# A scan's hand-written stage order: new letters, output finishes that run across stages, output transposes in the state's PSUM banks

## The chip, the cores and the metric

The kernel runs on one core of a Trainium2 chip. The metric is device microseconds of one execution. TensorE (PE) does the matrix products, VectorE (DVE) and ScalarE (ACT) read their results out of PSUM, GpSimd (POOL) works in SBUF alone, and SyncE (SP) issues nearly all DMAs. Each engine works its own instructions off in order and waits on semaphores for the others.

## The reference

One layer of a bidirectional mixer: 128 context tokens and 2048 latent tokens of width 1024. A norm and one input projection feed two head groups. Group B is a short gated convolution. Group A has 8 heads of 64 channels and runs a delta-rule state update once forward and once backward; the two results are added, normalised per head, gated, concatenated with group B and sent through one output projection.

```python
def step(S, inp):
    r_t, w_t, k_t, v_t, kk_t, a_t = inp
    s_kk = jnp.einsum('bdhij,bdhj->bdhi', S, kk_t)
    S = (S * w_t[..., None, :] - s_kk[..., :, None] * (kk_t * a_t)[..., None, :]
         + v_t[..., :, None] * k_t[..., None, :])
    return S, jnp.einsum('bdhij,bdhj->bdhi', S, r_t)
...
y = ys[:, 0] + jnp.flip(ys[:, 1], axis=1)
```

## The kernel before

`phase1` computes the projections and spills the operands of the scan to device memory, `phase2` is the scan, `phase3` the output projection. The change is in `phase2`.

The scan works on chunks of 64 tokens. A stage takes one pair of heads `p` and eight chunks per direction: group 0 is forward, group 1 backward. There are 17 stages: for each of four head pairs the four blocks b = 0 to 3 (the forward group takes block b, the backward group block 3 - b), and the context as stage 15. So stages 0 to 3 are b = 0 to 3 of the first head pair, 4 to 7 of the second, 8 to 11 of the third. Inside a stage `partS` makes eight steps. Step i multiplies the state with the chunk's matrix (psS, L1002), for group 0 and then group 1, and VectorE scales the new state into `sv` (L1015). This chain is serial: psS of the next step needs `sv` of this one.

Everything else in a stage is preparation for later stages or the end of earlier ones. It is cut into parts, which are generators or functions:

- `partL` loads the operands `rr` of a stage (1 MB per group, two buffers in all) four stages ahead.
- `partM`, three stages ahead, makes six pieces in the order of `MORD`: per group G with D (product psG, two masked copies to GA by VectorE, then `dg`), Q (transposes psQ, two ScalarE copies) and F (product psF, two ScalarE copies and two VectorE masks). All of them use a PSUM pool of two banks, and a piece takes both.
- `partI` transposes `dg` on VectorE (L852) and lets GpSimd solve the small triangular systems (L857 to L871).
- `partZ`, two stages ahead, transposes the solution on VectorE (L917, L920) and copies it into `zb` with four ScalarE copies. `partU`, one stage ahead, makes psU and psW with the ScalarE copies `bu` and the negated `zb`.
- `partW` and `partw`, one stage ahead, stack operands by eight ScalarE copies and load the rest. `partB` makes psX (eight ScalarE copies into `fs`) and then the chunk matrices psE with VectorE's masks into `E` (L965). `partm` takes the mean out of a new head pair's start state.
- `outputs` reads the upper half of a psS bank, after steps 3 and 7: a ScalarE copy (L719) at the first visit to `y`, which is in b = 0 and 1, a VectorE addition (L1032) at the second, in b = 2 and 3. Two output blocks are complete at the end of each b = 2 and b = 3.
- `finish` ends a completed block in pieces, one for each `f`: fetch `sg` and Square (ScalarE, L1063); the sum (VectorE, L1066); the root (ScalarE, L1068); reciprocal, multiply and the fetch of `q` (VectorE, L1070 and L1071); the transposes psT (TensorE, L1083) and their scaling (L1086); the addition (L1088) and the store to `mixT`.

What is written between the steps is set by strings: the eight strings of `ORDER`, one for each step, list the parts in the order in which they are issued after the step's own psS and `sv`. `b` is the rest of this stage's `partB`, `B` the start of the next one's; `M`, `W`, `U`, `I`, `Z`, `l`, `r`, `w`, `m`, `f` are the parts above. For stages 0 to 13 the instructions of TensorE, VectorE and ScalarE stand in exactly this order (`manual_schedule`). GpSimd's and SyncE's are placed by the planner, as are all of the last three stages, whose strings are in `LAST` and into which the output projection is woven.

PSUM has eight banks: two for `partM` and half of psX (`O.pm`), two for psU, psW, psX, psE and psT (`O.p2`), four for psS (`O.pS`), where two are taken at step 0 and two at step 4, each until `outputs` has read it.

Of the kernel before, what the change touches and what calls it, by code (L numbers as in the profile page):

```python
# [6 lines left out]
F32 = mybir.dt.float32  # L7
# [610 lines left out]


NST = 17  # L620
MORD = (("GD", 0), ("Q", 0), ("GD", 1), ("F", 0), ("Q", 1), ("F", 1))
ON_DVE = ""
LA = 3


ORDER = ("WbMUf", "WbMbMf", "fMUIlwf", "MfMr", "Bff", "Bfm", "ffZf", "Bf")
LAST = ("bUf", "bbWwf", "fWUf", "f", "Bff", "Bfm", "ffZf", "Bf")


def phase2(K):  # L630
    nc, tc, A, S = K.nc, K.tc, K.A, K.S
# [3 lines left out]
    B = Ctx()  # L635
    O = Ctx()
# [275 lines left out]
    def partZ(s, st):  # L912

        zr = st.zr = tl([128, 16, 32], "zr", 1, O.l1)
        zd = st.zd = tl([128, 16, 32], "zd", 1, O.l1)
        zb = B.zb
        r = V.transpose(zr[:].rearrange("p u (q h) -> p q h u", h=2), st.zt[:].rearrange("p q i -> p (q i)"))  # L917
        if O.scaled is not None:
            tc.add_manual_dep(r.ins, O.scaled.name, mybir.DependencyInfo(mybir.DependencyClass.NoSync, mybir.DependencyReason.DATA), reason="order")
        V.transpose(zd[:], zr[:])  # L920
        for r0, r1 in rows:
            copy("z", zb[r0, :, 0:32], zd[r0])
            copy("z", zb[r1, :, 32:64], zd[r1])
# [46 lines left out]
    sts = {}  # L970
    held = {}
    pend = []

    def partS(s, st, nxt):

        sp = {}
        for i in range(8):
            for gi, g in enumerate(st.g):
# [4 lines left out]
                p, c = g.units[u]  # L983
# [9 lines left out]
                m, q = (u % 2, u // 2) if ctx else (u // 4, u % 4)  # L993
# [23 lines left out]
                    if ctx and lastc:  # L1017
                        D(S["nst"][:, d, 2 * p:2 * p + 2, :], so[:])
                if i % 4 == 3:
                    outputs(g.units[0][0], g.blk, m, sp[gi])  # L1020
            yield

    def outputs(p, blk, m, ps):
# [16 lines left out]
    def finish(p, blk, y):  # L1040
# [31 lines left out]
        q = tl([128, 512], "w", 1)  # L1072
        fetch("q", q)
        yield
        pt = O.p2.tile([128, 512], F32, tag="s", name=f"psT{K.u()}")
        idm = B.idt[:]
        for i in range(4):
            if blk is None:
# [12 lines left out]
        else:  # L1091
            D(S["mixT"][p * 128:(p + 1) * 128, t0:t0 + 512], o[:])
        K.mixed[blk] = K.mixed.get(blk, 0) + 1
        yield

    K.mixed = {}

# [10 lines left out]
    def main():  # L1108
        setup_rest()
        run = lambda gen: [None for _ in gen]  # L1110
        partZ(0, sts[0])
        run(partW(0, sts[0]))
        partw(0, sts[0])
        partm(0, sts[0])
        run(first(2))
        partL(LA)
        run(partU(0, sts[0]))
        bb = partB(0, sts[0])
        for _ in range(3):
            next(bb)  # L1120
        partZ(1, sts[1])
        tail = iter(())
        order = tc.manual_schedule(engines={mybir.EngineType.PE, mybir.EngineType.DVE, mybir.EngineType.Activation})
        for s in range(NST):
            if s == 0:
                order.__enter__()
            if s == NST - 3:
                order.__exit__(None, None, None)
            st = sts.pop(s)
            nxt = sts.get(s + 1)  # L1130
            todo = [pend.pop(0) for _ in range(len(pend))]
            if s == NST - 3:
                O.pm.close()
                O.r2.close()
                O.r1.close()
                K.weights()
# [12 lines left out]
            for i, _ in enumerate(partS(s, st, nxt)):  # L1149
                next(tail, None)  # L1150
                for c in (ORDER if s < NST - 3 else LAST)[i]:
                    if c in gens:
                        next(gens[c], None)
                    elif c in "lr" and s + LA + 1 < NST:
                        partL(s + LA + 1, ("lr".index(c),))
                    elif c == "I" and s + LA < NST:
                        partI(s + LA, sts[s + LA])
                    elif c == "w" and nxt:
                        partw(s + 1, nxt)
                    elif c == "m" and nxt:  # L1160
                        partm(s + 1, nxt)
                    elif c == "Z" and s + 2 < NST:
                        partZ(s + 2, sts[s + 2])
                    elif c == "f":
                        while todo and next(todo[0], 1):
                            todo.pop(0)
            for f in todo:
                run(f)
        for f in pend:
            for _ in f:  # L1170
                pass
        for p in (O.pS, O.p2):
            p.close()
        K.rest(tail)
        for p in (O.l0, O.rI, O.r0):
            p.close()
# [190 lines left out]
```

## Time and profile before

| | us |
|---|---|
| median of 3 runs | 1763.87 (1762.28 to 1771.26) |
| profiled execution, its own time | 1767.54 |
| its span, first to last instruction | 1765.6 |
| up to the first psS of stage 0 | 1047.15 |
| stages 0 to 13 | 443.87 |
| stages 14 to 16 | 120.08 |
| from the last psS to the end | 154.50 |

The page of the profile names each group of instructions by line, engine, operation and the tiles it writes and reads. In the rows of a window view, each engine's busy time is followed by its number of instructions in brackets. In a row of the waits stand who waited, for whom, the time in total, how often and the longest. In a row of the timeline stand start, duration, engine, line and, in brackets, how long the engine was idle before and what ended it. A wait for several semaphores is put down to the one that came last.

### The profile page before, as it was taken

The page shows a single profiled execution, that of the slowest core. Times are in us where ns is not written, and L with a number is a line of the kernel's source. Part 1 is how long each engine was busy: PE and PEld are TensorE (multiplying, and loading weights), DVE is VectorE, ACT ScalarE, POOL GpSimd, SP SyncE. Part 2 cuts the span into 40 slices and gives each one's busy share as a digit, 9 for nine tenths or more (in the row PEclk, how much of TensorE's full clock was granted, in tenths as well). Part 3 has the DMA queues.
Part 4 walks back from the last instruction along what each step waited for, and adds up shares of the span by engine and source line. Part 5 has one row for each costly group of instructions (what it writes and reads, how often), then busy time and mean ns, then how long its engine had stood idle before and what let it go on. Part 6 is the DMA issues. An engine that isn't in the chain of part 4 may idle for free.

```text
span 1765.6 us, 42096 instructions
## 1 busy us (share of the span) xinstructions
PE 1588.2 (90%) x17364; PEld 1447.4 (82%) x17364; DVE 1126.3 (64%) x2099; ACT 776.9 (44%) x1539; POOL 586.4 (33%) x1053
## 2 busy tenths in 40 slices
PE   5998999999899999999999988978878878889998
PEld 2998899899888899989899977767767767677886
DVE  5998887545787626378854255776766766466433
ACT  4565644224444303255511155756556556442222
POOL 0122210001122100012208157876876776212221
PEclk8999999999899999999999968988989988989999
DMA  9788787565787744477785345455554654345442
GB/s 364 218 244 233 233 255 250 200 239 133 160 194 176 191 166 143 152 178 196 212 287 199 118 117 155 121 165 140 141 158 115 154 150 116 110 137 193 153 143 90
DMA packets 204271, 313.43 MB, mean 178 GB/s; under 512 B 58024, under 2 KB 147496, under 8 KB 190000
## 3 DMA queue, kind: packets, MB, share of 16 engines
q1 hardware_dynamic: 168496, 310.61, 58.5%
q10 hardware_dynamic: 35584, 0.14, 1.3%
q8 instruction: 136, 2.23, 0.5%
q14 instruction: 55, 0.45, 0.1%
HBM read 207.79 MB, written 102.91 MB: 176 GB/s over the span
## 4 chain that ended last, share of the span: by engine, by line
PE 44%; DVE 9%; ACT 6%; DMA 5%; issue 2%; POOL 0%; SPq 0%; DVEq 0%; ACTq 0%
PE psE L964 6%; PE psu L1240 3%; PE psu L1242 3%; DMA scr_ops<-sp 3%; PE psu L1241 3%; PE psS L1002 3%; PE psF L817 2%; ACT stf L717 2%; PE psX L950 2%; PE psG L817 2%; DVE ab L852 1%; PE psT L1083 1%; PE mmb L159 1%; PE mmb L160 1%; PE mmb L158 1%
## 5 line engine op out<-in xcount | busy, mean ns | idle before, releaser
L871 POOL TENSOR_TENSOR zt<-zt,ztmp 128x30 f32<-128x30 f32 (+7 forms) x510 | 202.3, 397 | 38.7
L868 POOL TENSOR_TENSOR ztmp<-ab,zt 128x60 f32<-128x60 f32 (+7 forms) x255 | 134.5, 527 | 19.2
L965 DVE TENSOR_TENSOR E<-psE,msk 128x512 f32<-128x512 f32 x136 | 93.0, 689 | 54.7 <-PE psE L964 54.3
L1002 PE MATMUL psS<-sv,E 128*64 128x64 f32 x2176 | 107.9, 242 | 18.7 <-DVE E L965 12.0
L1002 PEld LDWEIGHTS psS<-sv,E 128*64 128x64 f32 x2176 | 87.7, 150 | 41.5 <-DVE E L965 16.1
L314 POOL TENSOR_TENSOR shk<-rawl 128x384 f32<-128x384 f32 (+1 forms) x24 | 20.0, 833 | 279.8 <-ACT rawl L310 269.4
L717 ACT ACTIVATE stf<-psX 64x512 f32<-64x512 f32 x136 | 80.3, 590 | 35.5 <-PE psX L950 32.6
L1015 DVE TENSOR_TENSOR sv<-psS,pc 64x128 f32<-64x128 f32 x254 | 63.5, 274 | 45.5 <-PE psS L1002 44.8
L1303 POOL TENSOR_TENSOR z<-z,x 128x512 f32<-128x512 f32 x32 | 41.5, 1297 | 137.7 <-DVE z L1299 111.3
L158 PE MATMUL mmv<-h,w 128*128 128x384 f32 (+1 forms) x192 | 69.4, 361 | 18.9 <-ACT q1r L312 10.8
L817 PE MATMUL psF<-rr 64*64 64x128 f32 x1088 | 55.6, 312 | 19.5 <-ACT Q L719 14.7
L158 PE MATMUL mmg<-h,w 128*128 128x384 f32 (+1 forms) x192 | 64.3, 335 | 5.0 <-ACT ta L374 3.0
L159 PE MATMUL mmv<-h,w 128*128 128x384 f32 (+1 forms) x192 | 67.6, 352 | 0.0
L160 PE MATMUL mmv<-h,w 128*128 128x384 f32 (+1 forms) x192 | 67.4, 351 | 0.0
L195 POOL TENSOR_TENSOR hsls<-sq,hshs 128x384 fp32r<-128x384 f32 (+1 forms) x24 | 30.9, 1286 | 109.1 <-ACT hshs L194 40.2
L817 PEld LDWEIGHTS psF<-rr 64*64 64x64 f32 x1088 | 41.9, 151 | 29.0 <-ACT Q L719 16.6
L1083 PE MATMUL psT<-idt,y 128*64 128x128 f32 x272 | 26.7, 350 | 41.9 <-DVE y L1071 41.9
L158 PE MATMUL mmc<-h,w 128*128 128x384 f32 (+1 forms) x192 | 63.8, 332 | 0.3 <-DMA w<-scr_wsp 0.3
L159 PE MATMUL mmgb<-h,w 128*128 128x384 f32 (+1 forms) x192 | 63.6, 331 | 0.0
L159 PE MATMUL mmg<-h,w 128*128 128x384 f32 (+1 forms) x192 | 63.6, 331 | 0.0
L158 PE MATMUL mmgb<-h,w 128*128 128x384 f32 (+1 forms) x192 | 63.5, 331 | 0.0
L160 PE MATMUL mmg<-h,w 128*128 128x384 f32 (+1 forms) x192 | 63.4, 330 | 0.0
(313 smaller groups left out, 5247.2 us busy)
## 6 DMA issues: line engine op xcount, KB each, us to landing
w<-scr_wsp SPq DMA_DIRECT2D x68, 1024.0 KB, 6.0
scr_wsp<-w SPq DMA_DIRECT2D x34, 1024.0 KB, 6.2
rr<-scr_ops SPq DMA_DIRECT2D x32, 1024.0 KB, 5.7
scr_ops<-sp SPq DMA_DIRECT2D x160, 192.0 KB, 5.1
wr<-in_win SPq DMA_DIRECT2D x34, 512.0 KB, 6.9
x<-in_x SPq DMA_DIRECT2D x17, 512.0 KB, 3.8
wadas<-in_wada SPq DMA_DIRECT2D x8, 1024.0 KB, 14.6
stf<-scr_ops SPq DMA_DIRECT2D x32, 256.0 KB, 4.8
```

Of the source, the lines that this page charges most:

```text
L158: T.matmul(ps[:, :n], w[:, 0, k], hh[:, 0, k, :n], start=k == 0, stop=False)
L159: T.matmul(ps[:, :n], w[:, 0, k], hh[:, 1, k, :n], start=False, stop=False)
L160: T.matmul(ps[:, :n], w[:, 1, k], hh[:, 0, k, :n], start=False, stop=k == 7)
L717: P.activation(dst, src, AF.Copy, scale=-1.0)
L817: T.matmul(dst(h, a, er), w[hr_, u, :], x(hr_, u), start=True, stop=True)
L868: G.tensor_tensor(tv, ab[:, j:j + 2, j + 2:32].unsqueeze(1).broadcast_to((128, kn, 2, n)), zt[:, :kn, j:j + 2].unsqueeze(3).broadcast_to(( ...
L871: G.tensor_tensor(zt[:, :kn, j + 2:32], zt[:, :kn, j + 2:32], tv[:, :, r], ALU.subtract)
L964: T.matmul(pe[r, i, hd, :].rearrange("p (b t) -> p b t", b=2), g.lt[:, b, hd, us.start + k + i], g.rt[:, :, hd, us.start + k + i], start=T ...
L965: V.tensor_tensor(g.E[n][:, k:k + 2].rearrange("p a b c -> p (a b) c"), pe[:].rearrange("p a b c -> p (a b) c"), B.msk[:, ME[g.d]].unsquee ...
L1002: T.matmul(sp[gi][r, q, hd, :], g.E[n][:, k, hd, r], sv[:, u, hd, :], start=True, stop=True)
L1015: r = V.tensor_tensor(dst, sp[gi][0:64, q], B.pc[0:64, d, 2 * p:2 * p + 2, c:c + 1].broadcast_to((64, 2, 64)), ALU.mult)
L1240: T.matmul(ps[:], mh[:, n], hi[:, cs], start=start and n == 0, stop=False)
```

## The change

- `MORD`: the second Q comes ahead of the first F.
- `ORDER` and `LAST` are new. In the new strings `c` issues the four `zb` copies, which were the end of `partZ`, at step 0 of the following stage. `y` issues the outputs, which `partS` before issued by itself right after steps 3 and 7; they are collected in `made`. `N`, at step 7, takes the first piece of `partM` of the stage after, so that five `M` are left in a stage.
- `a`, at steps 1 and 5, opens one finish if none is open; each `f` moves it one piece on, and it may go on in the next stage. Before, the finishes of a stage were run one after the other inside the next stage, as fast as its `f` came. For the last three stages the old way stays.
- psT takes a bank of `O.pS` instead of `O.p2`.
- A last empty piece of `finish` is dropped.

```diff
-MORD = (("GD", 0), ("Q", 0), ("GD", 1), ("F", 0), ("Q", 1), ("F", 1))
+MORD = (("GD", 0), ("Q", 0), ("GD", 1), ("Q", 1), ("F", 0), ("F", 1))
-ORDER = ("WbMUf", "WbMbMf", "fMUIlwf", "MfMr", "Bff", "Bfm", "ffZf", "Bf")
-LAST = ("bUf", "bbWwf", "fWUf", "f", "Bff", "Bfm", "ffZf", "Bf")
+ORDER = ("cbWUMf", "fabMWbM", "IMUflw", "fMBfyr", "Bf", "fam", "fZ", "fByNf")
+LAST = ("cbUf", "bbWwf", "fWUf", "fy", "Bff", "Bfm", "ffZf", "Byf")
...
         V.transpose(zd[:], zr[:])
+
+    def partc(s, st):
+
+        zd, zb = st.zd, B.zb
         for r0, r1 in rows:
             copy("z", zb[r0, :, 0:32], zd[r0])
             copy("z", zb[r1, :, 32:64], zd[r1])
...
                 if i % 4 == 3:
-                    outputs(g.units[0][0], g.blk, m, sp[gi])
+                    made.append((g.units[0][0], g.blk, m, sp[gi]))
...
-        pt = O.p2.tile([128, 512], F32, tag="s", name=f"psT{K.u()}")
+        pt = O.pS.tile([128, 512], F32, tag="S", name=f"psT{K.u()}")
...
         K.mixed[blk] = K.mixed.get(blk, 0) + 1
-        yield
...
         partZ(1, sts[1])
+        coming = partM(LA, sts[LA])
+        next(coming)
         tail = iter(())
+        cur = []
...
-            todo = [pend.pop(0) for _ in range(len(pend))]
+            todo = []
+            if s >= NST - 3:
+                todo, pend[:], cur = cur + pend, [], []
...
-                        M=partM(s + LA, sts[s + LA]) if s + LA < NST else iter(()))
+                        M=coming)
...
-                    elif c == "f":
+                    elif c == "c" and nxt:
+                        partc(s + 1, nxt)
+                    elif c == "N":
+                        coming = partM(s + LA + 1, sts[s + LA + 1]) if s + LA + 1 < NST else iter(())
+                        next(coming, None)
+                    elif c == "y":
+                        while made:
+                            outputs(*made.pop(0))
+                    elif c == "a" and pend and not cur:
+                        cur = [pend.pop(0)]
+                        next(cur[0])
+                    elif c == "f" and s >= NST - 3:
                         while todo and next(todo[0], 1):
                             todo.pop(0)
+                    elif c == "f" and cur and next(cur[0], 1):
+                        cur = []
```

More of the change, by code (lines that the diff above doesn't have):

```diff
@@ L915, in partZ @@
         zd = st.zd = tl([128, 16, 32], "zd", 1, O.l1)
-        zb = B.zb
         r = V.transpose(zr[:].rearrange("p u (q h) -> p q h u", h=2), st.zt[:].rearrange("p q i -> p (q i)"))
@@ L972, in phase2 @@
     pend = []
+    made = []
     def partS(s, st, nxt):
@@ L1111, in main @@
         partZ(0, sts[0])
+        partc(0, sts[0])
         run(partW(0, sts[0]))
```

## The prediction

> **What bounds the kernel now.** I read the page first, then busy time cut at the first psS product of each stage, then TensorE's waits in that stretch, then the end of one stage in order of time.
>
> The page gives the span; the second view has one row for each of the 14 stages whose order is fixed by hand (0 to 13): stretch, length, busy time of PE, PEld, DVE, ACT, POOL, granted clock, DMA share, GB/s.
>
> ```profile
> span 1765.6 us, 42096 instructions
> ```
>
> ```profile
> 1047.15:1076.42 29.27, 25.77 (x643) 22.06 (x641) 17.96 (x37) 13.92 (x28) 20.77 (x47) 0.90 0.41 117
> 1076.42:1106.04 29.62, 25.84 (x645) 22.03 (x641) 18.06 (x38) 19.20 (x37) 23.24 (x54) 0.88 0.49 128
> 1106.04:1132.91 26.87, 23.57 (x640) 20.11 (x641) 20.79 (x42) 19.33 (x38) 20.48 (x47) 1.00 0.55 152
> 1132.91:1166.76 33.85, 26.75 (x672) 23.68 (x673) 26.55 (x54) 21.18 (x40) 29.13 (x62) 0.90 0.48 136
> 1166.76:1203.54 36.78, 28.82 (x674) 25.70 (x674) 23.31 (x47) 20.03 (x40) 26.60 (x57) 0.86 0.54 150
> 1203.54:1231.90 28.36, 24.69 (x644) 21.21 (x640) 18.48 (x39) 15.78 (x32) 16.87 (x40) 0.94 0.53 143
> 1231.90:1259.42 27.52, 23.58 (x641) 20.11 (x641) 20.58 (x42) 19.46 (x38) 22.02 (x51) 1.00 0.56 148
> 1259.42:1294.43 35.01, 27.52 (x673) 24.16 (x673) 26.49 (x55) 19.19 (x38) 29.19 (x62) 0.90 0.46 131
> ...
> sum 443.87, PE 367.21 PEld 318.46 DVE 304.36 ACT 261.10 POOL 327.69; mean PE 26.23 PEld 22.75 DVE 21.74 ACT 18.65 POOL 23.41
> ```
>
> The fixed stages take 443.9 us, and in them TensorE is busy 367.2: 76.7 us idle. The rows with 672 to 677 products (stages 3, 4, 7 here, and 8, 11, 12) hold two finishes and take 34 to 37 us; the others 27 to 30. No engine fills a stage: the order sets its length. The next view says which waits make up the idle time.
>
> ```profile
> PE psT L1083 <- DVE y L1071: 37.8, 11, 4.9
> PE psF L817 <- ACT Q L719: 14.7, 11, 2.5
> PE psS L1002 <- DVE E L965: 9.4, 14, 2.2
> PE psF L817 <- DVE GA L834: 3.6, 22, 0.2
> ```
>
> Half of it is psT, the transposes of a finished output. Here is why, at the end of stage 7 in order of time.
>
> ```profile
> 1282.45 2.44 ACT L717 ACTIVATE stf<-psX 64x512 f32<-64x512 f32 x4 [2.05 <-PE psX L950]
> ...
> 1283.93 0.69 PE L1002 MATMUL psS<-sv,E 128*64 128x64 f32 x16
> ...
> 1284.91 0.63 ACT L1063 ACTIVATE w<-y 128x512 f32<-128x512 f32 x1
> ...
> 1285.57 2.43 ACT L717 ACTIVATE stf<-psX 64x512 f32<-64x512 f32 x4
> ...
> 1288.02 0.30 ACT L1068 ACTIVATE yss<-yss,geps 128x8 f32<-128x8 f32 x1
> ...
> 1288.59 0.69 DVE L1071 TENSOR_TENSOR y<-y,yss 128x512 f32<-128x512 f32 x1
> ...
> 1289.43 1.98 PE L1083 MATMUL psT<-idt,y 128*64 128x128 f32 x16 [4.82 <-DVE y L1071]
> ```
>
> Square (L1063) stands behind four psX copies and the root (L1068) behind four more. The multiply comes at 1288.59, and psT, placed ahead of step 7's psS on TensorE, holds it up for 4.82 us. Its 16 products then took 1.98 us.
>
> **The change part by part.** Removed:
>
> *psT's wait, 37.8 us.* Square now opens at step 1 or 5, the sum follows one step later, root and multiply at step 3 or 7, and psT at step 4 or at the end of the next step 0. Between multiply and psT stand a psS and a psX or more, so the wait goes. No operation or DMA goes: sg fetch, q fetch and store still follow each other on SyncE.
>
> *psF behind the Q copies, 14.7 us.* Q of the second direction stood in step 3 behind the zb negations and output copies. It now goes out in step 1; ScalarE's copies of it follow four stack copies that are through by then. Gone.
>
> *psS behind the E masks, 9.4 us.* At the end of a stage the two output additions (L1032) and the two transposes stood ahead of the E masks on VectorE. The additions now stand behind them. Gone.
>
> *Slow clock.* Stages 2 and 6 were granted 1.00 and were busy 23.6. Fourteen such and twelve psT at 1.09 us (first row below) make 343.5; 367.2 were spent, so 23.7 us went to the lower clock. The rows show where it falls:
>
> ```profile
> 1277.03 1.09 PE L1083 MATMUL psT<-idt,y 128*64 128x128 f32 x16 [1.83 <-DVE y L1071]
> ```
>
> ```profile
> 1095.25 2.24 PE L817 MATMUL psF<-rr 64*64 64x128 f32 x32 [2.39 <-ACT Q L719]
> ```
>
> ```profile
> 1076.42:1090.00 13.58, 12.61 (x334) 10.89 (x334) 9.69 (x18) 9.63 (x18) 11.78 (x28) 1.00 0.29 66
> 1090.00:1098.00 8.00, 5.61 (x170) 4.86 (x164) 3.75 (x9) 4.28 (x10) 4.68 (x11) 0.76 0.75 200
> ```
>
> After a gap of 2.39 us the granted clock was 0.76 and 32 products took 2.24 us. The change removes these gaps but makes new ones at stage ends (below), of 2 to 4 us at most. I take half, 12 us; bounds 0 and 23.7.
>
> The Trainium skill (TensorE: Matmul & The Clock Gate, Part 1) puts the fall to half rate after an idle window of about 3.4 us. The trace has it after 2.39 us, so the measurement decides. By the page's rule all shorter gaps would be free and nearly the whole 23.7 would come back, for a time of about 1714.
>
> Added or left, from durations of these groups (busy us, mean ns after the bar):
>
> ```profile
> L965 DVE TENSOR_TENSOR E<-psE,msk 128x512 f32<-128x512 f32 x113 | 77.4, 690 | 44.3 <-PE psE L964 44.0
> L717 ACT ACTIVATE stf<-psX 64x512 f32<-64x512 f32 x112 | 66.1, 590 | 28.8 <-PE psX L950 26.4
> L1015 DVE TENSOR_TENSOR sv<-psS,pc 64x128 f32<-64x128 f32 x218 | 53.9, 274 | 29.4 <-PE psS L1002 28.8
> L834 DVE TENSOR_TENSOR GA<-psG,mkg 128x512 f32<-128x512 f32 x56 | 36.1, 686 | 9.2 <-PE psG L817 9.2
> L852 DVE STREAM_TRANSPOSE ab<-dg 128x1024 f32<-128x1024 f32 x14 | 28.7, 2049 | 0.0
> L719 ACT COPY y<-psS 64x512 f32<-64x512 f32 x30 | 17.4, 581 | 9.9 <-DVE sv L1015 9.5
> L1032 DVE TENSOR_TENSOR y<-psS,y 64x512 f32<-64x512 f32 x24 | 16.7, 694 | 0.7
> L837 DVE SCALAR_TENSOR_TENSOR dg<-GA,hm 128x256 f32<-128x256 f32 x28 | 15.2, 544 | 1.0
> L1071 DVE TENSOR_TENSOR y<-y,yss 128x512 f32<-128x512 f32 x12 | 8.8, 732 | 0.4
> L1070 DVE RECIPROCAL yss<-yss 128x8 f32<-128x8 f32 x12 | 2.3, 189 | 5.4 <-ACT yss L1068 5.3
> ```
>
> *VectorE's backlog at the stage end.* Step 7 now gives VectorE, after its E masks, the output additions (2 x 0.69, in stages that add), two GA masks (1.37) and dg (0.54) for the piece taken from the next stage, and reciprocal and multiply (0.92, where a second finish runs). The next psS0 needs only the first E mask, or the psG product about 1 us after the E products. VectorE is then late for the two sv scalings and the first E mask (0.55 + 0.69), on whose bank TensorE's psU waits; TensorE itself gets there in 2.5 us (psS and two E products). So a boundary loses the backlog less 1.26. Backlogs: stage 0 to 1 and each b=1 to b=2, 0.75 + 1.37 + 0.54 - 1.0 = 1.7; b=2 to b=3, the same with additions, 3.1; b=3 to b=0, 0.69 + 1.39 + 1.37 + 0.54 + 0.92 = 4.9; b=0 to b=1 with a finish, 3.5. Losses 0.4, 1.8, 3.6, 2.2, at 4, 3, 3 and 3 boundaries: 1.6 + 5.4 + 10.8 + 6.6 = 24.4. Bounds: 0, if other slack takes it up, and twice that, if one stage hands it on to the next.
>
> *F against F and Q.* F0 follows Q1 at a distance of one psS (0.6), its banks come free after Q1's last copy: 0.15. F1 waits for F0's masks, which now stand behind the 2.05 transpose of L852; TensorE has psW and psS in between: 0.4. Fourteen stages: 7.7.
>
> *psT in the state's banks.* Of four banks psS0 holds two until its output is read at step 3. psT of step 4 wants one: in the three stages where the output is a ScalarE copy behind four psX copies (4 x 0.59 + 0.58 = 2.9) and TensorE arrives after psS and psX (1.7), it waits 1.3: 3.9. Behind it on TensorE stands psS5, for which the state and so the whole stage wait. Above, a rival where psS itself is held; below, nothing.
>
> *At nothing.* The zb copies (2.5 us of ScalarE) leave step 6 for step 0, behind no wait, ahead of the stack copies and bu; bu is needed only by psW two steps on, and psU's products run 2.5 us into the stage; uncovered they cost 2.5 a stage. The first piece of stage 3 leaves the loop for the prologue: about 1 us there for 1 us here. Stages 14 to 16 are ordered by the planner and get three moved letters: bounds -4 and +4, taken as 0.
>
> **The sum.** Gains 37.8 + 14.7 + 9.4 + 12 = 73.9. Losses 24.4 + 7.7 + 3.9 = 36.0. Net 37.9: the profiled execution of 1767.5 (span 1765.6 and 1.9 around it) would become 1729.6. The median of the runs shown is 1763.9, 3.7 below that execution, so the forecast is 1726.
>
> **The rivals.**
>
> *The backlog is hidden* (24.4 comes back, gain 62): 1702. For it: VectorE is busy 304 of 444 us. Against: at the boundary its list is serial, and psU, Q and psS1 stand behind it.
>
> *psS held by a bank.* If banks are handed out in turn, psT shifts the turn and the second psS of step 4 gets a bank whose output copy stands behind four psX copies: 2.7 in each of six stages (b=0 and b=1 near a finish), 16 us: 1742. For: two more tenants in four banks. Against: at step 4 two banks are free.
>
> *VectorE paces the stage.* The backlog doubles, another 24.4: 1750. For it: DVE is busy 26.5 us in stages 3 and 7, nearly as long as TensorE. Against: 18 to 21 in the stages without finishes, which drain it.
>
> *Slower: psG ahead of psS0 waits for its load.* The next stage's first product now stands on TensorE before psS0, so a late rr load stops the state itself. SyncE's issues:
>
> ```profile
> 1273.26 6.91 SPq L798 DMA_DIRECT2D rr<-scr_ops  x2
> 1281.93 0.33 SPq L1092 DMA_DIRECT2D scr_mixT<-sg  x1
> 1287.03 0.33 SPq L1053 DMA_DIRECT2D sg<-scr_sg  x1
> ```
>
> ```profile
> rr<-scr_ops SPq DMA_DIRECT2D x32, 1024.0 KB, 5.7
> ```
>
> The load left 13.8 us into its stage and lands 5.7 later; psG needs it at about 23. Against it: 3 to 4 us to spare. For it: a store followed by an sg fetch held the queue 5.1 us, and the new order puts such a pair at step 1, before the load. A full load time lost in all 14 stages is 80, less 38: 1806. It decides once a stage loses 38 / 14 = 2.7 us.
>
> **How the numbers follow.** Forecast (1712 to 1736) 0.52; hidden backlog 0.16; held psS 0.15; pace of VectorE 0.09; late load 0.08. Range 1702 to 1757: it leaves out the late load, the tail of the doubled backlog and gains beyond 62. A measurement of this kernel can tell about 0.5% (8.8 us) from no change. Faster by more than that: the first three and a part of the fourth, 0.86; within it, 0.05; slower 0.09.
>
> **What would show it.** In the changed profile, psT's wait under 6 us in all, no psF wait on Q over 0.5, clock above 0.95 in most stages, finish stages of 28 to 32 us and the others of 25 to 27. My backlog is right if TensorE waits on E masks at steps 0 and 1 (psU or psE, not psS), some 20 us in all. It is wrong if psG shows a wait on a DMA, if psS at step 4 waits for L719 or L1032, or if the stages without a finish do not shrink.

## The result, and the profile after

| | before | after |
|---|---|---|
| median of 4 runs each, us | 1766.51 (1762.28 to 1771.26) | 1737.86 (1734.39 to 1741.1) |
| profiled execution, its own time | 1767.54 | 1734.39 |
| up to the first psS of stage 0 | 1047.15 | 1043.65 |
| stages 0 to 13 | 443.87 | 407.00 |
| stage 14 to the end | 274.58 | 281.65 |

The ratio is 0.9837, with a 95% interval of 0.9802 to 0.9872: the medians lie 28.7 us apart, the profiled executions 33.2. The forecast was a gain of 37.9. The stages whose order is written out by hand gave 36.9; the last three stages and the end took 7.1 back, and the prologue ran 3.5 shorter, which says little: over the runs told below it took between 1029.6 and 1047.2. The profiled execution of the kernel after is the fastest of its four runs, 3.5 below their median.

The window view of the kernel after, first in two parts (stages 0 to 13, and the rest), then stages 0, 3, 4 and 6. Columns as in the prediction: stretch, length, busy time of PE, PEld, DVE, ACT and POOL, granted clock, DMA share, GB/s.

```profile
1043.65:1450.65 407.00, 348.28 (x9123) 308.97 (x9121) 297.14 (x616) 264.81 (x507) 324.99 (x708) 0.94 0.54 149
1450.65:1732.30 281.65, 252.92 (x2016) 206.14 (x2016) 130.87 (x242) 89.83 (x188) 66.57 (x72) 0.95 0.43 136
...
1043.65:1068.26 24.61, 22.98 (x643) 19.84 (x641) 17.37 (x37) 16.64 (x33) 17.64 (x42) 1.00 0.57 150
...
1117.16:1147.21 30.05, 25.18 (x660) 22.30 (x657) 24.31 (x52) 19.64 (x38) 26.03 (x58) 0.94 0.55 152
1147.21:1180.33 33.12, 27.52 (x677) 24.77 (x673) 23.20 (x49) 18.21 (x37) 26.18 (x56) 0.90 0.55 156
...
1208.67:1233.24 24.57, 22.41 (x644) 19.82 (x640) 18.59 (x40) 17.95 (x35) 21.25 (x49) 1.00 0.55 153
```

The five stages with neither a finish nor the rest of one shrank from 27 to 30 us to 24.1 to 24.9, at a clock of 1.00; the others still run at 0.85 to 0.95. TensorE's busy time in the fixed stages fell by 18.9 us (367.2 to 348.3) and its idle time by 18.0 (76.7 to 58.7).

Not all of the 18.9 is the clock. In the trace the granted clock is either 1.00 or 0.50. It stood at 0.50 for 77.7 us of the fixed stages before and for 47.8 after, and TensorE was busy for 67.5 and 45.6 us of them. If a product takes up to twice as long there, at most half of that is extra time, 33.8 and 22.8 us, so the clock explains at most 11.0. About 1 us is the first piece of stage 3, now in the prologue. The rest shows at full clock too: in stage 6, granted 1.00 both times, TensorE was busy 23.6 us before and 22.4 after, psS 6.0 and 5.5 of it, psF 2.9 and 2.5. Why these products are shorter was not told apart.

What the idle time is now made of, in the same stretch (who waited, for whom, us in total, times, longest):

```profile
PE psU L934 <- DVE E L968: 20.3, 14, 2.5
PE psS L1006 <- DVE sv L1019: 12.6, 25, 3.0
PE psX L953 <- issue: 9.5, 8, 2.7
PE psS L1006 <- DVE E L968: 4.3, 4, 2.8
PE psF L817 <- issue: 3.3, 4, 1.4
PE psT L1087 <- ACT y L719: 2.9, 2, 1.5
PE psS L1006 <- issue: 2.4, 2, 1.9
...
PE psE L967 <- issue: 1.0, 2, 0.6
PE psT L1087 <- DVE y L1036: 0.5, 1, 0.5
```

Three lines matter. psT's wait, 37.8 before, is 3.4 in all, and psF's on Q (14.7) is gone. The largest wait is new: psU for the E masks, 20.3, the backlog of VectorE that the prediction priced at 24.4. And "issue" lines, in which TensorE waits for nothing the profile shows, add up to 16.2; before they were 4.4. The rows of the kernel before that were not shown yet, for the same stretch (1047.15 to 1491.02; its last 0.02 us take in one more wait of psS for the E masks than the 9.4 above):

```profile
PE psS L1002 <- DVE E L965: 11.2, 15, 2.2
...
PE psQ L817 <- issue: 2.1, 2, 1.7
PE psS L1002 <- DVE sv L1015: 1.2, 8, 0.2
...
PE psE L964 <- issue: 1.0, 1, 1.0
...
PE psF L817 <- issue: 0.7, 1, 0.7
PE psX L950 <- issue: 0.6, 1, 0.6
```

psU's wait has a row in each stage's order of time. Here it is for stages 2 to 6, whose boundaries the prediction had charged with 0.4, 1.8, 3.6, 2.2 and 0.4:

```profile
1095.64 1.20 PE L934 MATMUL psU<-zr,GA 32*32 32x32 f32 x64 [0.84 <-DVE E L968]
...
1121.26 1.20 PE L934 MATMUL psU<-zr,GA 32*32 32x32 f32 x64 [1.66 <-DVE E L968]
...
1152.17 1.05 PE L934 MATMUL psU<-zr,GA 32*32 32x32 f32 x31 [2.52 <-DVE E L968]
...
1184.50 1.20 PE L934 MATMUL psU<-zr,GA 32*32 32x32 f32 x64 [1.37 <-DVE E L968]
...
1211.63 1.20 PE L934 MATMUL psU<-zr,GA 32*32 32x32 f32 x64 [0.52 <-DVE E L968]
```

The ranking holds, boundary by boundary; the two largest charges, 3.6 and 2.2, were about half as much again as the waits (2.52 and 1.37).

The second line, psS for `sv`, is the state's own chain. The end of stage 7 in order of time:

```profile
1257.66 0.75 DVE L1090 SCALAR_TENSOR_TENSOR sg<-psT,gwh,sg 128x512 f32<-128x512 f32 x1 [3.17 <-PE psT L1087]
...
1258.72 0.67 DVE L1092 TENSOR_TENSOR sg<-sg,w 128x512 f32<-128x512 f32 x1
...
1260.96 0.47 DVE L1019 TENSOR_TENSOR sv<-psS,pc 64x128 f32<-64x128 f32 x2
...
1261.29 1.05 PE L1006 MATMUL psS<-sv,E 128*64 128x64 f32 x16 [1.96 <-DVE sv L1019]
```

The scaling and the addition of a finish stand on VectorE ahead of the state's `sv`, and between L1092 and L1019 lie the six short instructions of `partm`. TensorE, which psT no longer holds up, gets to psS before they are through.

### The profile page after: what moved, and what is told of

Read it like the earlier page. It is cut to its first block, busy times and chain, and to the rows that moved or that the text cites. A ratio compares the mean times of both kernels' runs of the same rounds, so it can differ in the third digit from the quotient of the medians.

```text
span 1732.3 us, 42127 instructions
## 1 busy us (share of the span) xinstructions
PE 1569.4 (91%) x17364; PEld 1437.7 (83%) x17364; DVE 1116.0 (64%) x2099; ACT 777.4 (45%) x1539; POOL 587.4 (34%) x1053
## 3 DMA queue, kind: packets, MB, share of 16 engines
q8 instruction: 136, 2.23, 0.6%
## 5 line engine op out<-in xcount | busy, mean ns | idle before, releaser
L1006 PE MATMUL psS<-sv,E 128*64 128x64 f32 x2176 | 101.8, 237 | 25.3 <-DVE sv L1019 12.7
L1006 PEld LDWEIGHTS psS<-sv,E 128*64 128x64 f32 x2176 | 83.8, 146 | 44.1 <-DVE sv L1019 17.5
L1019 DVE TENSOR_TENSOR sv<-psS,pc 64x128 f32<-64x128 f32 x254 | 63.2, 278 | 47.4 <-PE psS L1006 46.8
L158 PE MATMUL mmg<-h,w 128*128 128x384 f32 (+1 forms) x192 | 63.4, 330 | 4.5 <-ACT ta L374 2.5
L158 PE MATMUL mmc<-h,w 128*128 128x384 f32 (+1 forms) x192 | 63.9, 333 | 0.8 <-DMA w<-scr_wsp 0.8
L451 ACT ACTIVATE sg<-mmgb 128x384 f32<-128x384 f32 (+1 forms) x24 | 11.4, 474 | 118.2 <-PE mmgb L160 113.0
L159 PE MATMUL mmb<-h,w 128*128 128x384 f32 (+1 forms) x192 | 63.0, 328 | 0.0
L158 PE MATMUL mmu<-h,w 128*128 128x384 f32 (+1 forms) x192 | 62.9, 328 | 0.0
L159 PE MATMUL mmu<-h,w 128*128 128x384 f32 (+1 forms) x192 | 62.9, 328 | 0.0
L160 PE MATMUL mmc<-h,w 128*128 128x384 f32 (+1 forms) x192 | 62.9, 328 | 0.0
```

What stands on the lines that cost most here:

```text
L158: T.matmul(ps[:, :n], w[:, 0, k], hh[:, 0, k, :n], start=k == 0, stop=False)
L159: T.matmul(ps[:, :n], w[:, 0, k], hh[:, 1, k, :n], start=False, stop=False)
L160: T.matmul(ps[:, :n], w[:, 1, k], hh[:, 0, k, :n], start=False, stop=k == 7)
L1006: T.matmul(sp[gi][r, q, hd, :], g.E[n][:, k, hd, r], sv[:, u, hd, :], start=True, stop=True)
L1019: r = V.tensor_tensor(dst, sp[gi][0:64, q], B.pc[0:64, d, 2 * p:2 * p + 2, c:c + 1].broadcast_to((64, 2, 64)), ALU.mult)
```

## What the experiments were to tell apart

The theory after the result: the fixed stages went as forecast, because the finishes run across stages, with VectorE's backlog as the largest price; the missing gain is in the last three stages. Rivals: the new piece order or the psT bank made the gain; the additions behind the masks are not the backlog; the "issue" gaps come from the heavier DMA traffic at mid-stage.

Times of different chips are not compared: the kernel before took 1766.5 us on the first and 1756.7 to 1757.6 on the others, so every ratio is to it on the same chip. Lengths are of the one profiled execution. "Gaps" are the "issue" lines of TensorE in the fixed stages, "less gaps" the length without them (the time that a gap costs by a lower clock behind it stays in), and "rest" runs from stage 14 to the end.

| kernel | ratio (95%) | fixed stages | gaps | less gaps | rest |
|---|---|---|---|---|---|
| before | 1 | 443.9 | 4.4 | 439.5 | 274.6 |
| after | 0.9837 (0.9802 to 0.9872) | 407.0 | 16.2 | 390.8 | 281.7 |
| a1_bank | 0.9843 (0.9801 to 0.9886) | 416.5 | 23.3 | 393.2 | 274.4 |
| c2_tailbank | 0.9819 (0.9794 to 0.9844) | 411.8 | 20.5 | 391.3 | 276.2 |
| a2_finish | 0.9970 (0.9940 to 1.0000) | 432.4 | 13.4 | 419.0 | 279.4 |
| b2_finish | 1.0062 (1.0040 to 1.0085) | 454.2 | 4.1 | 450.1 | 275.3 |
| b1_pieces | 1.0031 (1.0007 to 1.0055) | 453.8 | 12.4 | 441.4 | 275.7 |
| a6_mord | 0.9998 (0.9967 to 1.0029) | 437.8 | 30.4 | 407.4 | 278.9 |
| a5_out | 0.9805 (0.9760 to 0.9850) | 397.2 | 16.7 | 380.5 | 280.5 |
| a3_shift | 0.9749 (0.9707 to 0.9790) | 385.1 | 17.9 | 367.2 | 281.6 |
| c1_both | 0.9709 (0.9679 to 0.9740) | 384.5 | 16.8 | 367.7 | 279.2 |
| a4_rlate | 0.9885 (0.9840 to 0.9929) | 406.9 | 16.0 | 390.9 | 280.2 |
| d2_late | one execution, 1731.47 us | 410.6 | 19.8 | 390.8 | 282.5 |
| d1_double | one execution, 1740.64 us | 416.0 | 14.5 | 401.5 | 278.9 |

The column "less gaps" says how far it can be trusted: after, a4_rlate and d2_late have the same engine order in the fixed stages, and c2_tailbank nearly so. Their lengths range from 406.9 to 411.8, without the gaps from 390.8 to 391.3.

## psT's bank, and the last three stages

**a1_bank.** psT back in the old pool, everywhere.

```diff
-        pt = O.pS.tile([128, 512], F32, tag="S", name=f"psT{K.u()}")
+        pt = O.p2.tile([128, 512], F32, tag="s", name=f"psT{K.u()}")
```

> The changed kernel with one part undone: psT takes a bank of O.p2 again, everything else as changed. Theory (the gain is the order of the finishes and of the pieces): psT at step 4 then waits for the copies of psX of the first group instead of the output's, both about 1 us after TensorE gets there, so the fixed stages stay within 5 us of the 407.0 of the changed kernel. Rival (the banks carry a good part of the gain, since psU, psE and psX share two banks): the fixed stages grow by 10 us or more, with psE, psU or psX waiting for psT's reader L1090.

The fixed stages were 9.5 us longer, which lies between what the theory and the rival expected; 7.1 of it are gaps, and 2.4 are left, with no wait of psE, psU or psX for L1090. So in the fixed stages the bank itself is worth little, and it isn't what made the gain. Whether it has a part in the gaps was not told apart. The rest of the kernel went back from 281.7 to 274.4.

**c2_tailbank.** The old pool in the last three stages alone.

```diff
+    sts_now = [0]
...
+        late = sts_now[0] >= NST - 3
-        pt = O.pS.tile([128, 512], F32, tag="S", name=f"psT{K.u()}")
+        pt = (O.p2 if late else O.pS).tile([128, 512], F32, tag="s" if late else "S", name=f"psT{K.u()}")
...
+            sts_now[0] = s
```

> The changed kernel, with psT in O.pS in the fixed stages alone and in O.p2 again in the last three. Theory (the 7.1 us that the changed kernel lost behind the fixed stages come from psT's bank there): last three stages plus end take 274 to 276 us instead of 281.7, the fixed stages stay at 405 to 410. Rival (the planner puts these stages in another order whenever anything ahead of them changes): they land anywhere from 274 to 284, and the first run's 274.4 was chance.

The rest took 276.2, just above the 274 to 276 of the theory, and the fixed stages 411.8 instead of 405 to 410, with 4.3 us more of gaps. With the old letters or those of the change, kernels with the old pool there need 274.4 to 276.2 (before, b1, b2, a1, c2); eight with the state's banks need 278.9 to 282.5. Only c1_both, told below, has the old pool with letters of its own and needs 279.2. So, with the letters of the change, the bank in stages 14 to 16 costs some 5 us, and the three moved letters by themselves next to nothing. TensorE's waits from stage 14 to the end show where: in the kernel after,

```profile
PE psT L1087 <- DVE y L1075: 7.5, 2, 6.2
PE psS L1006 <- DVE so L1019: 5.1, 3, 3.0
```

in a1_bank,

```profile
PE psT L1087 <- DVE y L1075: 4.9, 2, 4.5
...
PE psS L1006 <- DVE so L1019: 2.3, 1, 2.3
```

The two lines are 12.6 and 7.2 us in all; in the kernel before they were 6.7. These stages are ordered by the planner, and a bank free at another moment gave another order: from stage 14 to the end of the last psS 140.95 us instead of 120.08, and 140.70 instead of 154.50 from there to the end. TensorE makes 1457 products in the first of these stretches instead of 1363, so products of the output projection moved into the scan. That the last finish was so left with less to hide behind fits psT's longest wait (6.2 instead of 4.0), but was not tested.

## The finishes, alone and taken back

**a2_finish.** The kernel after, with the finishes of a stage run one after the other inside the next, at about the old places.

```diff
-ORDER = ("cbWUMf", "fabMWbM", "IMUflw", "fMBfyr", "Bf", "fam", "fZ", "fByNf")
+ORDER = ("cbWUMf", "bMWbMf", "IMUflwf", "MBfyr", "Bff", "fm", "ffZf", "BfyN")
...
-            todo = []
-            if s >= NST - 3:
-                todo, pend[:], cur = cur + pend, [], []
+            todo, pend[:] = list(pend), []
...
```

> The changed kernel with one part undone: the finishes run one after the other inside the next stage, with their letters where they were before (Square, root and multiply close together, psT right behind them at steps 3 and 6); the order of the pieces, the place of the outputs, of the zb copies and the bank of psT stay as changed. Theory (psT's wait and the slow clock behind it are the larger part): psT waits 25 to 40 us in all again, six stages go back to 33 to 37 us, the fixed stages to 430 to 445 (from 407.0). Rival (the pieces and the outputs' place carry it): the fixed stages stay below 420.

Ratio 0.997: nearly the whole gain is gone, 25.4 us of it in the fixed stages, as the theory had it. But psT's wait did not come back as 37.8:

```profile
PE psS L1006 <- DVE sv L1019: 23.4, 20, 3.8
PE psU L934 <- DVE E L968: 16.2, 14, 2.3
PE psT L1087 <- DVE y L1075: 12.7, 7, 2.9
```

Only 12.7 waits at psT; 10.8 more than after waits at psS for `sv`, and the busy time rose by 8.8, from 348.3 to 357.1.

**b2_finish.** The reverse: the kernel before, with nothing but the finishes spread across stages.

```diff
-ORDER = ("WbMUf", "WbMbMf", "fMUIlwf", "MfMr", "Bff", "Bfm", "ffZf", "Bf")
+ORDER = ("WbMUf", "faWbMbM", "MUIlwf", "fMMfr", "Bf", "Bfam", "fZ", "fBf")
...
+                    elif c == "a" and pend and not cur:
+                        cur = [pend.pop(0)]
+                        next(cur[0])
...
```

> The kernel before with one part of the change alone: one finish at a time, opened at steps 1 and 5, a piece for each f, running on across stages; order of the pieces, place of outputs and zb copies and psT's bank stay as before. Theory (this carries the larger part): psT's wait falls from 37.8 to below 8 us, the six long stages from 35.8 to 30 to 32 us, the fixed stages from 443.9 to 410 to 420. Rival (the finish only moves its wait to other places on VectorE and ScalarE): the fixed stages stay above 430.

Alone, the finishes gain nothing: that part of the theory fell. It is slower, 1.0062, its interval above 1:

```profile
PE psS L1002 <- DVE E L965: 27.1, 15, 3.4
PE psF L817 <- ACT Q L719: 27.0, 14, 3.3
PE psT L1083 <- ACT stf L717: 7.9, 6, 1.4
```

psT's wait went from 37.8 to 7.9 as meant, 29.9 less. But psF now waits 27.0 for Q instead of 14.7, psS 27.1 for the E masks instead of 11.2, and 5.9 for `sv` instead of 1.2: 32.9 more. ScalarE and VectorE are as late with Q and E as the old order makes them; TensorE, earlier there, waits for them instead of for psT. (Where the pieces of a finish stand in the old strings was chosen for this kernel; other places might do better.) Less gaps, the finishes alone cost 10.6, all the rest alone (a2_finish) gains 20.5, and both together gain 48.7. The waits of a fixed order don't add up: each is partly a cover for the next.

## The piece order

**b1_pieces.** The kernel before with the new `MORD` alone.

```diff
-MORD = (("GD", 0), ("Q", 0), ("GD", 1), ("F", 0), ("Q", 1), ("F", 1))
+MORD = (("GD", 0), ("Q", 0), ("GD", 1), ("Q", 1), ("F", 0), ("F", 1))
```

> The kernel before with one part of the change alone: the second Q ahead of the first F in the order of the pieces, nothing else. Theory (the wait of psF on ScalarE's Q copies is 14.7 us and goes with the order of the pieces): that wait falls below 3 us, the fixed stages from 443.9 to 430 to 438; psT's wait stays at 35 to 40. Rival (F1 now meets F0's masks behind the transposes of L852, and the finishes hold the same steps): the fixed stages stay within 4 us of 443.9.

In this kernel the letter `l`, which loads the next operands, comes ahead of group 0's F, so that F is computed from the operands of another stage and waits for their load. So it computes something else, and its ratio of 1.0031 says nothing on the piece order; it shows only that the new order can't be had with the old strings.

**a6_mord.** The kernel after with the old `MORD`.

> The changed kernel with one part undone: the pieces in the old order (first F ahead of the second Q), in the places that the new strings give them. Theory (the finishes pay only where no F waits for Q copies behind ScalarE's roots and negations): psF's wait on ACT Q comes back to 8 to 25 us, the fixed stages grow from 407 to 415 to 430. Rival (the places of the pieces in the steps matter, not their order): the fixed stages stay within 4 us of 407.

The edit is the reverse of the one above. Nothing is left of the gain (0.9998), yet not in the way that was expected: psF's wait on Q stayed away. With the new strings the second Q goes out in step 2 even in the old order, in step 3 before; so it is the strings, and not `MORD`, that take this wait away. What grew:

```profile
PE psX L953 <- issue: 24.8, 9, 4.0
...
PE psQ L817 <- DVE F L834: 4.2, 14, 0.3
```

Of 30.8 us more in the fixed stages, 14.2 are gaps, 14.1 is busy time at a lower clock (362.4 instead of 348.3, clock 0.91 instead of 0.94), and 4.2 is psQ behind the masks of F (smaller lines fell by the 1.7 that this is too much). Gaps in the middle of psX can themselves lower the clock (one that did is shown below); how much of the 14.1 is theirs was not told apart. In time, then, the piece order is as much needed for the gain as the finishes; that it works by the gaps and the clock is read from these rows, and why the old order has more gaps stays open.

## The additions at the stage end

**a5_out.** Outputs issued right after steps 3 and 7 again, as before, and so ahead of the E masks.

```diff
-                    made.append((g.units[0][0], g.blk, m, sp[gi]))
+                    outputs(g.units[0][0], g.blk, m, sp[gi])
```

> The changed kernel with one part undone: the outputs are issued right behind psS and sv of steps 3 and 7 again, ahead of the pieces, the psX copies and the E masks; everything else as changed. The finishes alone, put into the kernel before, gained nothing: psT's wait went, and psS's wait on the E masks rose from 9.4 to 25.2 us and psF's on the Q copies from 14.7 to 27.0. Theory (the finishes pay only where the outputs no longer stand ahead of the E masks): psS's wait on E comes back to 10 to 25 us and the fixed stages grow from 407 to 417 to 430. Rival (VectorE's list at the stage end has the same length either way): the wait only changes its name from psU to psS, and the fixed stages stay within 4 us of 407.

It went the other way. The fixed stages are 9.8 us shorter, 10.3 less gaps, though the ratio of 0.9805 does not tell it from after.

```profile
PE psU L934 <- DVE E L968: 14.2, 14, 1.7
...
PE psS L1006 <- DVE E L968: 7.2, 6, 3.2
```

psS waits 2.9 more for the masks, psU 6.1 less, and TensorE's busy time is another 6.0 shorter (342.3 instead of 348.3) at a clock of 0.97 instead of 0.94. Where the prediction put a gain of 9.4 for moving the additions behind the masks, the move takes 2.9 from psS and puts 6.1 on the next stage's psU.

**a3_shift.** The additions and the last piece of a finish go behind the first E masks of the next stage's step 0.

```diff
-ORDER = ("cbWUMf", "fabMWbM", "IMUflw", "fMBfyr", "Bf", "fam", "fZ", "fByNf")
-LAST = ("cbUf", "bbWwf", "fWUf", "fy", "Bff", "Bfm", "ffZf", "Byf")
+ORDER = ("cbyfWUMf", "fabMWbM", "IMUflw", "fMBfyr", "Bf", "fam", "fZ", "fBN")
+LAST = ("cbyUf", "bbWwf", "fWUf", "fy", "Bff", "Bfm", "ffZf", "Byf")
```

> The changed kernel with the outputs of step 7 and the last f of step 7 (reciprocal, multiply) moved behind the E masks of the next step 0. Theory (VectorE's list at the stage end is what psU waits for): the backlog shrinks by 1.39 and 0.92 us at six boundaries each, psU's wait on E falls from 20.3 us to 5 to 8, the fixed stages from 407.0 to 392 to 397. Rival (VectorE paces the stages anyway): the wait moves to psQ, psT or psS of step 1 and the fixed stages stay within 4 us of 407.

The window of its fixed stages, and their waits:

```profile
1039.03:1424.13 385.10, 334.48 (x9122) 294.77 (x9121) 296.89 (x616) 265.24 (x506) 327.59 (x708) 0.98 0.57 158
```

```profile
PE psS L1006 <- DVE sv L1019: 12.3, 24, 2.7
...
PE psU L934 <- DVE E L968: 7.5, 14, 0.7
```

psU's wait fell by 12.8 us, to half a microsecond a stage, and the clock rose to 0.98, which made another 13.8 of busy time good. The stages became 21.9 shorter, 23.6 less gaps, more than the 10 to 15 that were expected. So 12.8 of the backlog's 20.3 us were the additions and the finish's reciprocal and multiply, and its price was its waits together with the clock that they cost.

**c1_both.** a3_shift with the old pool in the last three stages.

> Both mends together: the outputs and the last f of step 7 behind the E masks of the next step 0, and psT in O.p2 in the last three stages. Theory: the two gains add, fixed stages at 383 to 389, last three stages plus end at 274 to 276, 0.967 to 0.973 of the time of the kernel before. Rival (the tail's gain is chance): no better than the 0.975 of the first mend alone.

The edit is those of a3_shift and c2_tailbank together. It is the fastest kernel here, 0.9709 (0.9679 to 0.9740), and beats both kernels of the case, before and after. The rest took 279.2 instead of the 274 to 276 expected; the letters in `LAST` are not those of c2_tailbank, and whether that is the reason was not told apart. By time it can't be told from a3_shift.

## The gaps without a releaser

TensorE stops in the middle of a group of products that needs nothing new. Stage 7 of the kernel after, TensorE and then the two operand loads:

```profile
1251.53 0.65 PE L953 MATMUL psX<-F,zb 64*64 64x128 f32 x13
1254.35 1.35 PE L953 MATMUL psX<-F,zb 64*64 64x128 f32 x19 [2.16 <-issue]
```

```profile
1247.32 0.36 SPq L798 DMA_DIRECT2D rr<-scr_ops  x1
...
1250.15 0.36 SPq L798 DMA_DIRECT2D rr<-scr_ops  x1
```

The DMA view has a queue for the instructions themselves. In the 7.0 us up to 1251.9 (the first fence), it moved nothing; in the next 1.2 us (the second) one packet. The columns are packets, MB and share of the 16 engines.

```profile
q1 hardware_dynamic: 802, 1.51, 94.9%
```

```profile
q1 hardware_dynamic: 215, 0.44, 98.1%
q8 instruction: 1, 0.02, 5.7%
```

That packet starts at 1251.95, takes 1.1 us, and TensorE goes on 1.3 us after its end. It is so with every gap over 0.3 us in all runs: each ends 1.2 to 1.8 us after the end of a packet of this queue. And each begins at the end of a block: if TensorE's instructions are counted in order from the start of the program, all 187 gaps in the fixed stages of the 14 profiles stand a multiple of 256 instructions apart.

Such a gap can cost more than itself. Here the granted clock (third column from the right) fell behind it to 0.50 for 3.41 us:

```profile
1251.18:1254.59 3.41, 1.25 (x37) 0.94 (x35) 3.20 (x7) 2.21 (x4) 3.10 (x5) 1.00 1.04 377
1254.59:1258.00 3.41, 3.41 (x47) 3.08 (x41) 0.34 (x1) 2.36 (x4) 2.78 (x9) 0.50 0.71 261
```

When is a packet late? The fixed stages of the 14 profiles hold 981 whole blocks of 256 instructions. In the first 2 us of 455 of them the data queues kept the DMA engines busy for less than half of the time, and no gap follows any of these, though TensorE used up 333 of them in under 6 us. In the first 2 us of 387 others the engines were over 90% busy, and 180 gaps follow: behind 145 of the 174 that TensorE used up in under 5 us, and behind none of the 71 that lasted over 7. So nearly every gap (all but 7) came with both, full DMA engines and a TensorE that ran through its block without long waits. This is what the runs have in common, not yet an experiment. Three experiments tried to change the traffic.

**a4_rlate** moves the letter `r`, the second operand load, from step 3 to step 6.

```diff
-ORDER = ("cbWUMf", "fabMWbM", "IMUflw", "fMBfyr", "Bf", "fam", "fZ", "fByNf")
+ORDER = ("cbWUMf", "fabMWbM", "IMUflw", "fMBfy", "Bf", "fam", "fZr", "fByNf")
```

> The changed kernel with the second rr load moved from step 3 to step 6. In the changed kernel TensorE has 14 gaps of 0.4 to 2.7 us inside groups of products, 16.2 us in all, that wait for nothing the profile shows; each ends 1.3 to 1.6 us after a 16 KB packet of the instruction queue has landed, and most come while the two rr loads are on the way. Theory (the instruction packet is late because it queues behind the rr loads): with one load less at that time the gaps at steps 3 to 5 fall to below 8 us in all, and what is left moves towards step 7; the fixed stages lose 3 to 8 us. Rival (TensorE simply uses up instructions faster than they come, whatever the loads do): the gaps keep their total and their place.

SyncE's order is the planner's, and it issued the load as early as before. The cause was not changed, and nothing follows.

**d2_late** makes ScalarE, whose order is fixed, issue that load at step 6 (beside the string of a4_rlate).

```diff
-                D(g.rr[:, 0:4].rearrange("p k u t -> p k (u t)"), src.rearrange("k p t -> p k t"))
+                (nc.scalar.dma_start if gi and s > LA else D)(g.rr[:, 0:4].rearrange("p k u t -> p k (u t)"), src.rearrange("k p t -> p k t"))
```

> The changed kernel with the second rr load issued by ScalarE at step 6, where it stands in the fixed order; in the earlier try the planner had put SyncE's load back to its old time. Theory (loads make the instruction packet late): the gaps at steps 3 to 5 fall below 10 us, some appear at steps 7 and 0. Rival (consumption alone): total and place as before.

The load left 19 to 31 us into its stage instead of 15 to 22. Gaps of 19.8 instead of 16.2, 16.0 of them still at steps 3 to 5 (15.2 after), three others at steps 0 and 7: the second load by itself is not their cause.

**d1_double** adds an extra copy of 1 MB in device memory at step 2 of each stage; nothing reads it.

```diff
+                        if c == "l":
+                            nc.scalar.dma_start(K.S["again"][:], S["ops0"][:, 0:128, 0:512])
...
```

> The changed kernel with one more transfer of 1 MB in each stage, from device memory to device memory, issued by ScalarE right behind the first rr load; its result is not used. In the changed kernel TensorE has 16.2 us of gaps inside groups of products, each ending 1.3 to 1.6 us after a 16 KB packet of the instruction queue. Theory (the packet that is due at steps 2 to 4 comes late because the loads are on the way): with more traffic the gaps grow to 24 us or more and stay at steps 3 to 5. Rival (consumption alone): 12 to 20 us as before.

The gaps did not grow (14.5). The extra copy left 13.7 to 19.8 us into its stage. In stages 0, 2, 3, 4, 9 and 10 the packet ahead of the gap at step 3 had started by then, so these test nothing. In stages 1, 6, 7, 8 and 12 the copy left 0.3 to 3.7 us ahead of it, and the gaps at steps 3 and 4 are 7.4 us in all against 7.0 in the kernel after; in the last four the engines had been full for the 3 us before the packet without the copy, too. So a further transfer adds little there. The stages became 9.0 longer all the same, among it 5.0 more of psS waiting for `sv`. No run emptied the engines at a place where a gap stands, so that their being full is the cause, and in what way, stays open.

## Why the prediction was right, and where it was not

The forecast was 1726 (1712 to 1736 for its own case, range 1702 to 1757); measured 1737.9, inside the range and 2 us beyond its own case. The mechanism, finishes out of the way against a backlog of VectorE, is the one that the waits show; the gain at the median is 9.2 us smaller. Of these, 1.0 is missing in the fixed stages and 7.1 in the rest, the prologue gave 3.5 back, and 4.6 come from the profiled executions, which lie further apart than the medians (the one after is the fastest of its runs). By its steps, for the fixed stages:

| step | forecast | measured |
|---|---|---|
| psT's wait gone, less what its new bank costs | 37.8 - 3.9 | 37.8 to 3.4: 34.4 |
| psF behind Q | 14.7 | 14.7, by the strings |
| psS behind the E masks | 9.4 | 11.2 to 4.3: 6.9 |
| psF behind the masks of G | not priced | 3.6 |
| slow clock | 12 | at most 11.0 |
| TensorE's busy time apart from the clock | not priced (about 1 of it put at nothing) | 7.9 |
| backlog at the stage end | -24.4 | -20.3, at psU |
| F against F and Q | -7.7 | none |
| psS behind `sv` | not priced | 1.2 to 12.6: -11.4 |
| gaps without a releaser | not priced | 4.4 to 16.2: -11.8 |
| sum | 37.9 | 35.0 from these rows, 36.9 by length |

So the sum is better than its terms, and that is luck. Two losses were missing, 23.2 in all: the state's own chain, which the finish's scaling and addition now hold up on VectorE (shown for the end of stage 7), and the gaps. What hid them: "F against F and Q" was charged 7.7 and shows no line, the backlog was charged 4.1 too much, and two gains had no price, 3.6 and 7.9.

*Slow clock, 23.7 at most*: the size that was taken, 12, about fits, but the bound does not hold. The prediction took the 23.6 us of stages 2 and 6 as TensorE's busy time at full clock. In the kernel after, the five stages at 1.00 need 22.4 to 23.0, and a3_shift's 334.5 in all lies below the 343.5 that were taken as the floor. That gaps of 2 to 4 us at the stage ends would go on lowering the clock held: nine of the 14 stages are below 1.00, and the gap of 2.16 us shown above was enough. So the shorter gaps were not free, and the 1714 that went with that was not reached.

*Stages 14 to 16, "bounds -4 and +4, taken as 0"*: this is the step that took the time out of its own case. They cost 7.1. The prediction costed the moved letters, which are free, and gave psT's bank no price where the planner sets the order; c2_tailbank gave 5.5 of the 7.1 back.

*psF behind the Q copies*: the wait went as forecast, and because the second Q goes out earlier, as the prediction says. a6_mord shows that the new strings do this without `MORD`.

*psS behind the E masks, "Gone"*: the additions did stand ahead of the masks, but behind them they are in the way of something else. The wait fell from 11.2 to 4.3, and a5_out shows that the move bought 2.9 of this with 6.1 more of psU's wait. So one move stood in the sum as a gain of 9.4 and, with its 1.39 us at two kinds of boundary, inside the loss of 24.4. Its balance by the length of the fixed stages is a loss of about 10, which the ratios are too wide to confirm.

*The sum as a sum*: b2_finish and a2_finish show that its terms are not independent. Taking psT's wait alone gives nothing; the gain needs the whole order. The sum came out because the change took the next waits away together with the first.

*The signs named beforehand*: psT under 6 held (3.4), no psF wait on Q held, some 20 us at psU held (20.3). Clock above 0.95 "in most stages" did not: five of the 14 reach it, five have 0.94 to 0.95, four 0.85 to 0.90. Stages with finishes took 30.0 to 34.7 (forecast 28 to 32), those without and not behind one 24.1 to 24.9 (25 to 27); b = 1, which shares its finishes with b = 0, 28.3 to 30.2.

*The rivals*: hidden backlog (1702) fell, psU waits 20.3. psS held by a bank (1742) fell: no line has psS waiting for an output copy, though its time is the nearest to the median. VectorE pacing (1750) fell, since the backlog did not double, though a3_shift shows that it was the largest thing left. The late load fell in its form: psG waits for no DMA. But its premise was partly right. The first load leaves 18.5 us into stages 4 and 8 instead of 13.8 to 14.0 (within 1 us of before in stages 3, 6 and 7), and over all 32 loads the median landing is 7.2 us after the issue instead of 5.7:

```profile
rr<-scr_ops SPq DMA_DIRECT2D x32, 1024.0 KB, 7.2
```

## What to carry to other kernels

In an order written out by hand, a wait that is removed uncovers the next late producer behind it: before costing a move, look at what that instruction's engine and the two instructions behind it would wait for if it were ready, and count a moved operation at its new place as well as at its old one. Work that nobody needs soon, such as an output addition, belongs behind the next operation on its engine that somebody does wait for, even across a stage's boundary. A buffer pool that is changed for one part of a program is shared by the parts that a planner orders, and is to be costed there too.

## What the hardware showed that was not expected

TensorE can run out of instructions. The page counts 136 packets of the instruction queue in the kernel after, as in the one before:

```profile
PE 1569.4 (91%) x17364; PEld 1437.7 (83%) x17364; DVE 1116.0 (64%) x2099; ACT 777.4 (45%) x1539; POOL 587.4 (34%) x1053
...
q8 instruction: 136, 2.23, 0.6%
```

2.23 MB in 136 packets are 16 KB each. In the stretch shown above such a packet came while the other queue kept the DMA engines 95 to 98% busy, and TensorE stood still; gaps of this kind last up to 4.0 us and make 4.4 us in all before, 16.2 after, 30.4 in a6_mord. It differs between kernels with the same or nearly the same engine order (16.0 to 20.5), and hides differences of a few microseconds between them. The Trainium skill (Runtime: NRT & Kernel Launch, Instruction fetch mechanics) says that instructions are fetched in blocks of 16 KiB, 256 each, and that the cost of crossing a block is mostly hidden. The count agrees, 34,728 products and weight loads being 135.7 blocks of 256; the cost was not hidden here. That full DMA engines are what delays the packets fits all 14 profiles, but was not shown by a change to them.
